# Recurrent branch of a hybrid layer: the chain's products on the full array instead of on half and quarter tiles

## The chip, the cores and the metric

One core of a Trainium2 chip. TensorE (PE) multiplies, VectorE (DVE), ScalarE (ACT) and GpSimd (POOL) work on what it leaves in PSUM, SyncE (SP) issues most transfers. The metric is the device time of one launch in microseconds; the time before is the median of three runs, 2056.92 us (2055.39 to 2056.93).

## The reference, cut to what matters

One layer of a decoder trunk of width 2048 over 288 tokens: 32 sample tokens (8 sequences of 4) and one prompt of 256. The norm of x goes through one input projection. Its columns feed two branches: RWKV-7 time mixing with 32 heads of 64 channels, and sliding-window attention. Gates merge the branches, and an output projection, a squared-ReLU MLP of width 8192 and a last norm follow. For each head the time mixing updates a 64 x 64 state S token by token:

```
sa  = S a_t                              (what is to be removed)
S   = S * w_t + v_t k_t^T + sa b_t^T     (decay, new value, removal)
y_t = S r_t
```

The outputs y are group-normalised per head, gain a bonus term and are gated. The states and the shifted columns of the last tokens are outputs as well. All inputs and outputs are float32.

## The kernel before

Channels lie on partitions, in 16 tiles of 128 (two heads each), and tokens along the free axis. `dense()` makes one output tile: a half tile of weights is loaded, split in two float32r parts by ScalarE (`whi`, L141) and VectorE (`wlo`, L142), and every contraction tile takes three products with 288 columns (L170 to L172). A half tile is thus 24 products. `whi` and `wlo` have two buffers each.

The recurrence goes in chunks of 64 prompt tokens, 4 of them, so that TensorE can do it. Two channel tiles are a group (GP = 2), and there are 8 groups. `pair()` prepares one channel tile: decayed and scaled copies of r, k, a and b (`T`, `bk`), coefficients within a chunk (L563), sample tokens (L579, L590). `chain()` works on a group: first VectorE inverts 32 x 32 triangular blocks by a recurrence on `A` and `utmp` (L625, L627), whose result goes out to DRAM and comes back (L641, `Y`, L659); small products on 32 x 32 tiles finish the inverse (`YT`, L664, L683); then the chunks follow one another:

- `za` (L721): states and values times the removal part of `T`, copied to `zs` by ScalarE (L723);
- `sa` (L732): the inverse times `zs`; VectorE scales it into `Z` (L735);
- `sn` (L739): the change of state; VectorE adds it to the state (L746) and decays it (L747), and ScalarE puts the result into the next chunk's `Z` (L751);
- the outputs gather in a PSUM bank `y` through L728 (old state) and L742 (within the chunk).

After four chunks the rows of y are centred (L702 to L705), squared, and scaled by GpSimd (L764), transposed back to channels (L771), and the sample states are updated (L787, L788). `finish()` adds bonus and gate (L809 to L814); its gate product (L184 to L186) uses the only bank of the small products (`ps_lo`).

The products of the chain take the two heads apart: 64 rows or 64 columns of the array for each head, as tiles of 128 x 64 and 64 x 64; L563 uses 64 x 128. Each of their instructions is two records in the trace, since the operands are float32.

The main loop (L327) issues `pair()` for one channel tile after another and after each of its steps three steps of side work (SIDE_STEPS), which is chain and finish of earlier groups; attention has its own pace. The order on every engine is then set once, when the program is built: a scheduler takes instructions of all these streams as their inputs and buffers come free. On the chip each engine's queue runs in that order.

Of the kernel before, what the change touches and what calls it, by code (L numbers as in the profile page):

```python
# [8 lines left out]
F32 = mybir.dt.float32  # L9
# [13 lines left out]
GP = 2  # L23
# [17 lines left out]
def _col_tiles():  # L41
    """Columns of w_in, tile by tile, and the index of each tile."""
# [30 lines left out]
def _consts():  # L73
# [5 lines left out]
    out["gmask"] = np.concatenate([s < t, s <= t], 1)  # L79
# [3 lines left out]
    out["smask"] = np.concatenate([same & (sp < tp), same & (sp <= tp)], 1)  # L83
    out["bmask"] = (sp // 4 == np.arange(8)[None, :])
# [40 lines left out]
class Builder:  # L125
# [21 lines left out]
    def weights(self, src):  # L147
        """One half tile [128, 1024] of weights, split in two float32r parts."""
# [29 lines left out]
    def lora(self, parts, out=None):  # L178
        """psum[128, NT] = sum of the parts (whi, wlo, xhi, xlo)."""
# [14 lines left out]
    def rstd(self, ps, out):  # L194
        """1 / sqrt(mean + eps) from the sums of squares in psum."""
# [6 lines left out]
    def build(self):  # L202
# [10 lines left out]
        self.ps_ch = self.pool("ps_ch", 2, PSUM)  # L213
        self.ps_y = self.pool("ps_y", 1, PSUM)
# [21 lines left out]
    def phase1(self, c1, ph):  # L236
# [9 lines left out]
        nc.gpsimd.dma_start(out=self.mu, in_=io["mu"])  # L246
        self.lhi = p1.tile([128, 4, NT], F32R, name="lhi")
        self.llo = p1.tile([128, 4, NT], F32R, name="llo")
        # the first tiles take x times the norm's weight, and the token's factor afterwards
        with ExitStack() as st:  # L250
# [9 lines left out]
            for q in range(8):  # L260
# [11 lines left out]
                # sums of squares: the first on the tensor engine, which waits for x anyhow  # L272
# [39 lines left out]
        nc.gpsimd.dma_start(out=self.sinks, in_=io["sinks"].partition_broadcast(128))  # L312
        self.srow = p1.tile([128, 4], F32, name="srow")
        nc.gpsimd.dma_start(out=self.srow, in_=io["srow"])
# [3 lines left out]
        self.GR = [p1.tile([128, 2, NCH, C], F32, name=f"GR{i}") for i in range(4)]  # L318
        for t in self.GR:
            nc.gpsimd.memset(t[64:128, 0], 0.0)  # L320
            nc.gpsimd.memset(t[0:64, 1], 0.0)
# [5 lines left out]
        for ct in range(KT):  # L327
# [9 lines left out]
            if 1 <= ct <= 4:  # L337
                # past rows of the sample V window
# [8 lines left out]
        # the rest of the gates, and the output projection over the first half of the channels  # L347
# [40 lines left out]
    def advance(self, side, n):  # L388
        """n steps of the side work; an item waits for the attention that it needs."""
# [8 lines left out]
    def shift(self, ps, name, tag, rstd=None):  # L398
        """Token shift of one tile of projected columns; also keeps the last tokens."""
# [35 lines left out]
    def group_begin(self, g):  # L435
# [5 lines left out]
        G.T, G.GB, G.GR, G.BKT, G.GS, G.Zs, G.bv, G.bkS = ([None] * GP for _ in range(8))  # L441
# [5 lines left out]
    def pair(self, G, p):  # L447
# [6 lines left out]
        # decay  # L454
# [22 lines left out]
        # a, k and the removal vectors  # L477
# [8 lines left out]
        # squared norms: by token for the chunks, along the columns for the sample tokens  # L486
# [23 lines left out]
        # scaled operands: rows of the second head hold k before b  # L510
        bk = ew.tile([128, NCH, 2, C], F32, name="bk")
        bks = ew.tile([128, 2, NS], F32, name="bks")
        T = G.T[p] = gp.tile([128, 2, NCH, 128], F32, name="T", bufs=4)
        ars = ew.tile([128, 2, NS], F32, name="ars", bufs=2)
        a8 = lambda i: ars[:, i, :].rearrange("p (b t) -> p b t", t=TS)
        hs = [slice(0, 64), slice(64, 128)]
        for h in range(2):
            r = hs[h]
# [605 lines left out]
```

## Time and profile before

| | |
|---|---|
| median of three runs | 2056.92 us |
| span of the profiled execution | 2052.3 us |
| TensorE busy | 1985.0 us (97%), 15732 records |
| VectorE busy | 1307.2 us (64%) |
| ScalarE busy | 948.5 us (46%) |
| GpSimd busy | 323.7 us (16%) |
| split of weights, L142, on VectorE | 621.3 us, 504 of 1234 ns |
| TensorE's waits for that split, 88 to 1140 us | 12.8 us, 19 of them, the longest 1.3 |

The recurrent branch and attention lie between some 88 and 1100 us, beside the dense products of the input projection; the output projection and the MLP follow. All times are of one profiled execution, whose span is 4.6 us under the median of the runs. The ends of products are modelled, so a price is read from start to start, over the dense products on both sides.

### The profile page before, as it was taken

Reading aid. Unit: us, or ns where it says so; the run is one execution under the profiler, and the core shown is the slowest. Engines: PE = TensorE matmul, PEld = TensorE weight load, DVE = VectorE, ACT = ScalarE, POOL = GpSimd, SP = SyncE. Lnnn points to the kernel's source line nnn. Section 1 sums busy time; section 2 is a strip of 40 time slices with the busy share of each in tenths; the row PEclk is TensorE's granted clock in tenths of the full one; section 3 lists DMA queues with packets and bytes.
Section 4 is the critical chain, followed back from the end, with each engine's and each line's share of the span. In section 5 each row is a group of like instructions: output and inputs, shape, how many; then the busy total and the mean of one; then the engine's idle time right before and its main releaser. Section 6 shows DMA issues by size and latency. Waiting matters only on the chain.

```text
span 2052.3 us, 39981 instructions
## 1 busy us (share of the span) xinstructions
PE 1985.0 (97%) x15732; PEld 1869.8 (91%) x15732; DVE 1307.2 (64%) x2594; ACT 948.5 (46%) x1801; POOL 323.7 (16%) x551
## 2 busy tenths in 40 slices
PE   6999999999999999899999999999999999999996
PEld 5998898988888888798888999999999999999996
DVE  8667768677686786977766684544554444444455
ACT  5545544545454454545444455433443344335442
POOL 6322213232141321414022000000000000000000
PEclk9999999999999999999999999999999999999998
DMA  5545455354553444445446655455545555555552
GB/s 195 162 145 166 124 157 162 115 167 130 151 167 111 143 148 147 135 141 161 127 137 197 192 163 166 159 173 166 165 158 172 164 165 162 167 165 165 165 166 96
DMA packets 156764, 319.21 MB, mean 156 GB/s; under 512 B 58208, under 2 KB 80768, under 8 KB 156512
## 3 DMA queue, kind: packets, MB, share of 16 engines
q1 hardware_dynamic: 156480, 316.61, 48.4%
q8 instruction: 124, 2.03, 0.4%
q14 instruction: 64, 0.52, 0.1%
q0 software_dynamic: 96, 0.05, 0.1%
HBM read 300.11 MB, written 18.52 MB: 155 GB/s over the span
## 4 chain that ended last, share of the span: by engine, by line
PE 72%; DVE 10%; DMA 3%; issue 2%; ACT 1%; POOL 1%; SPq 1%; DVEq 0%; ACTq 0%; POOLq 0%
PE mm L172 21%; PE mm L170 21%; PE mm L171 21%; DVE wlo L142 2%; DVE A L627 1%; DVE utmp L625 1%; PE gr L563 1%; PE y L742 1%; PE y L728 1%; DMA A<-scr 1%; PE gr L590 1%; PE ch L721 1%; PE ch L739 1%; PE ch L732 1%; PE lo L905 0%
## 5 line engine op out<-in xcount | busy, mean ns | idle before, releaser
L142 DVE TENSOR_TENSOR wlo<-raw,whi 128x1024 fp32r<-128x1024 f32 x504 | 621.3, 1234 | 461.0 <-ACT whi L141 455.9
L141 ACT CAST whi<-raw 128x1024 fp32r<-128x1024 f32 x504 | 528.2, 1050 | 728.8 <-PE mm L171 664.3
L172 PE MATMUL mm<-xhi,wlo 128*128 128x288 f32 x2304 | 694.6, 302 | 13.4 <-DVE wlo L142 13.3
L170 PE MATMUL mm<-xhi,whi 128*128 128x288 f32 x2304 | 690.8, 300 | 5.3 <-ACT bt L412 2.9
L171 PE MATMUL mm<-xlo,whi 128*128 128x288 f32 x2304 | 688.0, 299 | 0.0
L172 PEld LDWEIGHTS mm<-xhi,wlo 128*128 128x128 f32 x2304 | 435.2, 189 | 32.6 <-DVE wlo L142 18.2
L170 PEld LDWEIGHTS mm<-xhi,whi 128*128 128x128 f32 x2304 | 434.8, 189 | 17.0 <-issue 6.0
L171 PEld LDWEIGHTS mm<-xlo,whi 128*128 128x128 f32 x2304 | 434.7, 189 | 11.0 <-issue 8.7
L171 PE MATMUL mm<-ul,whi 128*128 128x288 f32 x1024 | 302.0, 295 | 0.0
L170 PE MATMUL mm<-uh,whi 128*128 128x288 f32 x1024 | 301.9, 295 | 0.0
L172 PE MATMUL mm<-uh,wlo 128*128 128x288 f32 x1024 | 301.5, 295 | 0.0
L172 PEld LDWEIGHTS mm<-uh,wlo 128*128 128x128 f32 x1024 | 192.7, 188 | 0.0
L170 PE MATMUL mm<-mhi,whi 128*128 128x288 f32 x640 | 189.6, 297 | 2.9 <-ACT mhi L144 1.8
L171 PEld LDWEIGHTS mm<-ul,whi 128*128 128x128 f32 x1024 | 192.2, 188 | 0.0
L170 PEld LDWEIGHTS mm<-uh,whi 128*128 128x128 f32 x1024 | 191.9, 187 | 0.0
L171 PE MATMUL mm<-mlo,whi 128*128 128x288 f32 x640 | 189.7, 296 | 0.2 <-DVE mlo L145 0.2
L172 PE MATMUL mm<-mhi,wlo 128*128 128x288 f32 x640 | 189.1, 296 | 0.7 <-DVE wlo L142 0.7
L1019 POOL TENSOR_TENSOR h<-h,rstd 128x288 f32<-128x288 f32 x5 | 4.9, 1013 | 910.7 <-DVE rstd L199 910.7
L170 PEld LDWEIGHTS mm<-mhi,whi 128*128 128x128 f32 x640 | 120.4, 188 | 4.2 <-ACT mhi L144 2.1
L172 PEld LDWEIGHTS mm<-mhi,wlo 128*128 128x128 f32 x640 | 121.0, 189 | 1.1 <-DVE wlo L142 1.0
L171 PEld LDWEIGHTS mm<-mlo,whi 128*128 128x128 f32 x640 | 120.7, 189 | 1.4 <-issue 0.8
L625 DVE TENSOR_TENSOR utmp<-A,U 108x84 f32<-108x84 f32 (+12 forms) x240 | 66.3, 276 | 18.7 <-DMA A<-scr 11.6
(303 smaller groups left out, 2344.1 us busy)
## 6 DMA issues: line engine op xcount, KB each, us to landing
raw<-win SPq DMA_DIRECT2D x216, 512.0 KB
raw<-wup SPq DMA_DIRECT2D x128, 512.0 KB
raw<-wdn SPq DMA_DIRECT2D x128, 512.0 KB
raw<-wout SPq DMA_DIRECT2D x32, 512.0 KB
S<-wkv SPq DMA_DIRECT2D x32, 256.0 KB
lraw<-lora SPq DMA_DIRECT2D x32, 128.0 KB
o_wkvs<-S SPq DMA_DIRECT2D x16, 256.0 KB
U<-scr SPq DMA_DIRECT2D x24, 144.0 KB
```

Source lines behind the costliest of these rows:

```text
L141: nc.scalar.copy(out=dst_hi, in_=src)
L142: nc.vector.tensor_tensor(out=dst_lo, in0=src, in1=dst_hi, op=ALU.subtract)
L170: nc.tensor.matmul(ps[:, :NT], lhsT=a, rhs=hi, start=(i == 0), stop=False)
L171: nc.tensor.matmul(ps[:, :NT], lhsT=a, rhs=lo, start=False, stop=False)
L172: nc.tensor.matmul(ps[:, :NT], lhsT=b, rhs=hi, start=False, stop=(i == len(kts) - 1))
L563: nc.tensor.matmul(grs[h][:, c, :], lhsT=bk[hs[h], c, :, :].rearrange("p a b -> p (a b)"), rhs=T[hs[h], h, c, :], start=True, stop=True)
L590: nc.tensor.matmul(rt[hs[h]], lhsT=ars[hs[h]].rearrange("p a b -> p (a b)"), rhs=S0[hs[h]], start=True, stop=True)
L625: nc.vector.tensor_tensor(out=tv, in0=A[:, 0:n, j:j + 1].broadcast_to([3 * NU, n, m]), in1=U[:, j:j + 1, j + 1:32].broadcast_to([3 * NU, n ...
L627: nc.vector.tensor_tensor(out=A[:, 0:n, j + 1:32], in0=A[:, 0:n, j + 1:32], in1=tv, op=ALU.add)
L721: nc.tensor.matmul(za[hs[h], p, :], lhsT=G.T[p][:, h, c, 0:64], rhs=Zc[:, h, p, :], start=True, stop=True)
L728: nc.tensor.matmul(y[half, cp, p, h, :], lhsT=G.T[p][:, h, c, 64:128], rhs=Zc[:, h, p, :], start=(cp == 0 and p == 0 and h == 0), stop=False)
L732: nc.tensor.matmul(sa[hs[h], p, :], lhsT=YT[hs[h], p, c, :], rhs=zs[hs[h], p, :], start=True, stop=True)
```

## The change

Every operand of the two heads becomes one block operand with zeros where the other head would be, and one product on the full array serves both. `T` holds removals and outputs of one chunk side by side, so that one product gives `za` and the old part of the outputs. `BG` holds the scaled b and k of a chunk beside the coefficients of the outputs, so that one product gives the change of state and the new part of the outputs. `YT`, `YS`, `abd`, `bbd` and `cbd` are block operands for the inverse, the sample tokens and the sample outputs. The outputs no longer gather in PSUM: `za` and `sn` each have a part of them, ScalarE copies one (`y1`, L760) and VectorE adds the other (`yt`, L761). The bank that was `y` becomes a third bank of the chain. GpSimd clears the new operands. Three small loads go from GpSimd's queue to SP's. The products L664 and L683 stay as they are. Lines from 576 on are 8 to 13 higher after the change. The core of the diff:

```diff
-        self.ps_ch = self.pool("ps_ch", 2, PSUM)
-        self.ps_y = self.pool("ps_y", 1, PSUM)
+        self.ps_ch = self.pool("ps_ch", 3, PSUM)
...
-        nc.gpsimd.dma_start(out=self.mu, in_=io["mu"])
+        nc.sync.dma_start(out=self.mu, in_=io["mu"])
...
+        self.BG = [p1.tile([128, NCH, 2, 2, C], F32, name=f"BG{i}") for i in range(4)]
...
+        for t in self.YT + self.YS + self.abd + self.bbd + [self.cbd]:
+            nc.gpsimd.memset(t, 0.0)
...
-        T = G.T[p] = gp.tile([128, 2, NCH, 128], F32, name="T", bufs=4)
+        T = G.T[p] = gp.tile([128, 2, NCH, 2, C], F32, name="T", bufs=4)
...
+            nc.gpsimd.memset(T[hs[1 - h], h], 0.0)
...
-        nc.scalar.copy(out=BKT, in_=tr)
+        for h in range(2):
+            nc.scalar.copy(out=BG[:, :, h, h, :], in_=tr[:, :, h, :])
...
-            za = bank64()
+            za = four(bank()[:, 0:GP * 128])
             for p in range(GP):
                 for h in range(2):
-                    nc.tensor.matmul(za[hs[h], p, :], lhsT=G.T[p][:, h, c, 0:64], rhs=Zc[:, h, p, :], start=True, stop=True)
+                    nc.tensor.matmul(za[:, p, h, :], lhsT=G.T[p][:, h, c].rearrange("q a b -> q (a b)"), rhs=Zc[:, h, p, :], start=True, stop=True)
             zs = gp.tile([128, GP, 64], F32, name="zs")
-            nc.scalar.copy(out=zs, in_=za)
+            for h in range(2):
+                nc.scalar.copy(out=zs[hs[h]], in_=za[hs[h], :, h, :])
             yield 0
             sa = bank64()
             for p in range(GP):
-                for h in range(2):
-                    nc.tensor.matmul(y[half, cp, p, h, :], lhsT=G.T[p][:, h, c, 64:128], rhs=Zc[:, h, p, :],
-                                     start=(cp == 0 and p == 0 and h == 0), stop=False)
...
-                    nc.tensor.matmul(sa[hs[h], p, :], lhsT=YT[hs[h], p, c, :], rhs=zs[hs[h], p, :], start=True, stop=True)
+                nc.tensor.matmul(sa[:, p, :], lhsT=YT[:, p, c].rearrange("q h t -> q (h t)"), rhs=zs[:, p, :], start=True, stop=True)
...
-                    nc.tensor.matmul(sn[hs[h], p, :], lhsT=G.BKT[p][:, c, hs[h]], rhs=Zc[:, h, p, :], start=True, stop=True)
-            for p in range(GP):
-                for h in range(2):
-                    nc.tensor.matmul(y[half, cp, p, h, :], lhsT=G.GR[p][:, h, c, :], rhs=Zc[:, h, p, :], start=False,
-                                     stop=(c >= 2 and p == GP - 1 and h == 1))
-            yield 0
+                    nc.tensor.matmul(sn[:, p, h, :], lhsT=G.BG[p][:, c, h].rearrange("q a b -> q (a b)"), rhs=Zc[:, h, p, :], start=True, stop=True)
             Sn = gp.tile([128, GP, 64], F32, name="Sm", bufs=2)
-            nc.vector.tensor_tensor(out=Sn, in0=sn, in1=Sm, op=ALU.add)
+            for h in range(2):
+                nc.vector.tensor_tensor(out=Sn[hs[h]], in0=sn[hs[h], :, h, :], in1=Sm[hs[h]], op=ALU.add)
...
+            y1 = gp.tile([128, GP, 64], F32, name="y1")
+            for h in range(2):
+                o = hs[1 - h]
+                nc.scalar.copy(out=y1[o], in_=za[o, :, h, :])
+                nc.vector.tensor_tensor(out=yt[half, cp, :, h, :], in0=sn[o, :, h, :], in1=y1[o], op=ALU.add)
             yield 0
...
-            for h in range(2):
-                nc.tensor.matmul(sn[hs[h]], lhsT=G.bkS[p][hs[h]], rhs=zm[hs[h]], start=True, stop=True)
+            nc.tensor.matmul(sn, lhsT=G.bkS[p], rhs=zm, start=True, stop=True)
```

The order of the queues changes with it. First place: TensorE's queue in the chain of the sixth group, before the change. `mm` is a dense product, `ch` and `y` are banks of the chain; a number belongs to one tile in memory.

```order
L170 MATMUL mm_11783<-xhi_93,whi_11786 128x288
L171 MATMUL mm_11783<-xlo_94,whi_11786 128x288
L739 MATMUL ch_11206<-Z_8434,BKT_8931 64x64 x2
L739 MATMUL ch_11206<-Z_8434,BKT_9798 64x64 x2
L742 MATMUL y_11043<-Z_8434,GR2_566 64x64 x2
L742 MATMUL y_11043<-Z_8434,GR3_567 64x64 x2
L172 MATMUL mm_11783<-xhi_93,wlo_11787 128x288
L170 MATMUL mm_11783<-xhi_93,whi_11786 128x288
```

After the change, the last two chunks of the same group, from the last dense product on:

```order
L173 MATMUL mm_12033<-xhi_90,wlo_12067 128x288
L731 MATMUL ch_10948<-Z_8566,T_8916 128x64 x2
L731 MATMUL ch_10948<-Z_8566,T_9784 128x64 x2
L738 MATMUL ch_10956<-zs_10953,YT1_574 128x64 x2
L746 MATMUL ch_11033<-Z_8566,BG2_563 128x64 x2
L746 MATMUL ch_11033<-Z_8566,BG3_564 128x64 x2
L731 MATMUL ch_11049<-Z_8567,T_8916 128x64 x2
L731 MATMUL ch_11049<-Z_8567,T_9784 128x64 x2
L738 MATMUL ch_11057<-zs_11054,YT1_574 128x64 x2
L746 MATMUL ch_11106<-Z_8567,BG2_563 128x64 x2
L746 MATMUL ch_11106<-Z_8567,BG3_564 128x64 x2
L782 MATMUL ch_11207<-cst_89,cen_10755 128x128 x2
```

Before, dense products stand on both sides of each step; after, two chunks and the transposes of the normalised rows stand behind one another, and the next dense product comes only behind L795, L783, L665, L675, L192 and a gate product.

Second place: VectorE's queue in the chain of the seventh group, before the change. `A` and `utmp` are the recurrence of the next group's inverse, `wlo` the split of a half tile of weights, `S` and `am` belong to attention.

```order
L142 TENSOR_TENSOR wlo_13297<-raw_13294,whi_13296 128x1024
L877 SCALAR_TENSOR_TENSOR S_13117<-cst_92,gr_13120 128x384
L627 TENSOR_TENSOR A_12935<-A_12935,utmp_13172 108x6x13
L735 TENSOR_TENSOR Z_10091<-ch_12614,RH_10093 64x128 x2
L878 TENSOR_REDUCE am_13118<-S_13117 128x2
L879 TENSOR_REDUCE am_13118<-S_13117 128x2
L625 TENSOR_TENSOR utmp_13175<-A_12935,U_12934 108x84
L882 TENSOR_SCALAR am_13118<-am_13118,sinks_558 128x2 x2
L627 TENSOR_TENSOR A_12935<-A_12935,utmp_13175 108x7x12
L883 TENSOR_SCALAR am_13118<-am_13118 128x4
L625 TENSOR_TENSOR utmp_13178<-A_12935,U_12934 108x77
L142 TENSOR_TENSOR wlo_13327<-raw_13324,whi_13326 128x1024
```

After the change, from the last split of weights ahead of the place at which that group's last chunk ends without dense products between its steps:

```order
L143 TENSOR_TENSOR wlo_13067<-raw_13064,whi_13066 128x1024
L642 TENSOR_TENSOR A_12571<-A_12571,utmp_12685 108x4x19
L740 TENSOR_TENSOR Z_10208<-ch_12282,RH_10210 64x128 x2
L640 TENSOR_TENSOR utmp_12688<-A_12571,U_12570 108x90
L642 TENSOR_TENSOR A_12571<-A_12571,utmp_12688 108x5x18
L640 TENSOR_TENSOR utmp_12691<-A_12571,U_12570 108x85
L642 TENSOR_TENSOR A_12571<-A_12571,utmp_12691 108x5x17
L640 TENSOR_TENSOR utmp_12694<-A_12571,U_12570 108x80
L749 TENSOR_TENSOR Sm_12292<-ch_12287,Sm_12191 64x128 x2
L761 TENSOR_TENSOR yt_11971<-ch_12287,y1_12297 64x2x64 x2
L642 TENSOR_TENSOR A_12571<-A_12571,utmp_12694 108x5x16
L750 TENSOR_TENSOR Sm_12292<-Sm_12292,DE_10209 128x128
```

Before, two splits stand 11 rows apart, with the recurrence, attention and the chain between them; after, the next split stands 69 rows behind the first row here, and in between are 37 instructions of the recurrence, the group's last chunk, its normalisation and the sample states. TensorE's queue there holds, between two dense products, L731, L738, L746, L782, L795, L783, L795, L665, L675, L605 and the first scores of attention (L845 to L881).

## Rows read from the trace of the kernel before

**Rows 1.** by stretch: length, then for each engine busy us and records; PEclk, DMA, GB/s

```profile
88.00:1140.00 1052.00, 1020.88 (x8567) 909.82 (x8567) 775.64 (x1909) 507.23 (x1163) 271.87 (x470) 0.99 0.48 148
...
1400.00:1600.00 200.00, 200.00 (x1505) 200.00 (x1504) 95.68 (x110) 83.27 (x111) 0.00 (x0) 1.00 0.51 166
```

**Rows 2.** timeline of TensorE, line 732: start, us, engine, line, out<-in, tile, sizes, records

```profile
1062.38 0.29 PE L171 MATMUL mm<-xlo,whi 128*128 128x288 f32 x1
1062.60 0.45 PE L732 MATMUL ch<-zs,YT 64*64 64x64 f32 x8
...
1063.22 0.29 PE L170 MATMUL mm<-xhi,whi 128*128 128x288 f32 x1
```

**Rows 3.** timeline of TensorE, lines 739 and 742

```profile
1080.37 0.29 PE L170 MATMUL mm<-xhi,whi 128*128 128x288 f32 x1
1080.59 0.45 PE L739 MATMUL ch<-Z,BKT 128*64 128x64 f32 x8
1080.88 0.63 PE L742 MATMUL y<-Z,GR 128*64 128x64 f32 x8
...
1081.68 0.29 PE L172 MATMUL mm<-xhi,wlo 128*128 128x288 f32 x1
```

**Rows 4.** timeline of TensorE, line 563

```profile
846.74 0.29 PE L172 MATMUL mm<-xhi,wlo 128*128 128x288 f32 x1
846.96 1.16 PE L563 MATMUL gr<-T,bk 64*128 64x128 f32 x8
...
848.28 0.29 PE L171 MATMUL mm<-xlo,whi 128*128 128x288 f32 x1
```

**Rows 5.** timeline of TensorE, line 787

```profile
309.15 0.29 PE L171 MATMUL mm<-xlo,whi 128*128 128x288 f32 x1
309.37 1.08 PE L787 MATMUL ch<-zm,bkS 64*64 64x512 f32 x4
...
310.61 0.29 PE L170 MATMUL mm<-xhi,whi 128*128 128x288 f32 x1
```

**Rows 6.** timeline of TensorE, line 902 on the full array

```profile
410.24 0.30 PE L171 MATMUL mm<-xlo,whi 128*128 128x288 f32 x1
410.38 0.71 PE L902 MATMUL gr<-cst,S 128*128 128x128 f32 x5
...
411.06 0.30 PE L170 MATMUL mm<-xhi,whi 128*128 128x288 f32 x1
```

**Rows 7.** costliest groups by line: busy us, mean ns of one, idle before

```profile
L142 DVE TENSOR_TENSOR wlo<-raw,whi 128x1024 fp32r<-128x1024 f32 x504 | 621.3, 1234 | 461.0 <-ACT whi L141 455.9
L627 DVE TENSOR_TENSOR A<-A,utmp 108x84 f32<-108x84 f32 (+12 forms) x240 | 68.0, 283 | 4.5
L625 DVE TENSOR_TENSOR utmp<-A,U 108x84 f32<-108x84 f32 (+12 forms) x240 | 66.3, 276 | 18.7 <-DMA A<-scr 11.6 <-issue 1.7 <-DMA U<-scr 0.9
L751 ACT COPY Z<-Sm 64x128 f32<-64x128 f32 x48 | 14.3, 298 | 21.7 <-DVE Sm L747 21.1
...
L746 DVE TENSOR_TENSOR Sm<-ch,Sm 128x128 f32<-128x128 f32 x32 | 9.2, 287 | 13.0 <-PE ch L739 12.7
```

**Rows 8.** chain that ended last, 600 to 640 us: start, us, what

```profile
599.43 1.78 SPq L641
...
604.01 0.43 DVE X L659
```

**Rows 9.** timeline of all engines in the tail

```profile
1096.54 1.08 PE L955 MATMUL lo<-pP,vp 128*128 128x32 f32 x8 [1.76 <-DMA vp<-cv]
...
1102.49 0.69 DVE L702 TENSOR_REDUCE gst<-y 128x8 f32<-128x512 f32 x1
...
1105.29 0.71 PE L170 MATMUL mm<-mhi,whi 128*128 128x288 f32 x2 [1.85 <-ACT mhi L144]
...
1110.61 1.26 POOL L764 TENSOR_TENSOR cen<-cen,gst 128x640 f32<-128x640 f32 x1 [1.70 <-DVE gst L763]
```

**Rows 10.** by stretch, in the tail; columns as in rows 1

```profile
1098.60:1102.00 3.40, 3.14 (x26) 2.70 (x27) 1.96 (x8) 0.41 (x1) 0.00 (x0) 0.51 0.44 125
```

More of the change, by code (lines that the diff above doesn't have):

```diff
@@ L78, in _consts @@
     s, t = (p % 64)[:, None], np.arange(64)[None, :]
-    out["gmask"] = np.concatenate([s < t, s <= t], 1)
+    out["gmask"] = np.concatenate([s < t, s <= t, s < t], 1)
     sp = (p % 32)[:, None]
@@ L83, in _consts @@
     out["smask"] = np.concatenate([same & (sp < tp), same & (sp <= tp)], 1)
+    out["sel"] = (p % 64)[:, None] == 32 + tp
     out["bmask"] = (sp // 4 == np.arange(8)[None, :])
@@ L440, in group_begin @@
         G.RH = gp.tile([128, GP, NCH], F32, name="RH", bufs=3)
-        G.T, G.GB, G.GR, G.BKT, G.GS, G.Zs, G.bv, G.bkS = ([None] * GP for _ in range(8))
+        G.T, G.GB, G.BG, G.GS, G.Zs, G.bv, G.bkS = ([None] * GP for _ in range(7))
         G.R = gp.tile([128, GP, 64], F32, name="R", bufs=3)
@@ L671, in chain @@
         for p in range(GP):
-            for h in range(2):
-                nc.tensor.matmul(sa[s32[h], p, :], lhsT=YS[s32[h], p, :], rhs=zs[s32[h], p, :], start=True, stop=True,
-                                 tile_position=(h * 64, h * 64))
+            nc.tensor.matmul(sa[:, p, :], lhsT=YS[:, p].rearrange("p h a -> p (h a)"), rhs=zs[:, p, :], start=True, stop=True)
         for p in range(GP):
@@ L682, in chain @@
                 for h in range(2):
-                    nc.tensor.matmul(qq[s32[h], p, c, :], lhsT=Pm[k32[h], p, c, :], rhs=YT[k32[h], p, c, 32:64], start=True, stop=True,
+                    nc.tensor.matmul(qq[s32[h], p, c, :], lhsT=Pm[k32[h], p, c, :], rhs=YT[k32[h], p, c, h, 32:64], start=True, stop=True,
                                      tile_position=(h * 64 + 32, h * 64))
         for h in range(2):
-            nc.scalar.copy(out=YT[s32[h], :, :, 32:64], in_=qq[s32[h]])
+            nc.scalar.copy(out=YT[s32[h], :, :, h, 32:64], in_=qq[s32[h]])
         yield 0
@@ L689, in chain @@
         for p in range(GP):
-            for h in range(2):
-                nc.tensor.matmul(yp[hs[h], p, :], lhsT=G.GS[p][hs[h]].rearrange("p a b -> p (a b)"), rhs=G.Zs[p][hs[h], :], start=True, stop=True)
+            nc.tensor.matmul(yp[:, p, :], lhsT=flat(G.GS[p]), rhs=G.Zs[p], start=True, stop=True)
         ys = gp.tile([128, GP, 64], F32, name="ys", tag="zs")
@@ L713, in chain @@
         nc.gpsimd.memset(Z[0][64:128, 1], 0.0)
-        y = self.ps_y.tile([128, NCH // 2, GP, 2, 64], F32, name="y")
+        yt = gp.tile([128, NCH // 2, GP, 2, 64], F32, name="yt")
+        four = lambda t: t.rearrange("q (p h i) -> q p h i", p=GP, h=2)
         for c in range(NCH):
@@ L763, in chain @@
         nc.vector.reciprocal(out=rs, in_=rs)
-        nc.gpsimd.tensor_tensor(out=cen, in0=cen, in1=rs.unsqueeze(2).broadcast_to([128, NR, 64]), op=ALU.mult)
+        n4 = 4 * GP
+        nc.gpsimd.tensor_tensor(out=cen[:, 0:n4], in0=cen[:, 0:n4], in1=rs[:, 0:n4].unsqueeze(2).broadcast_to([128, n4, 64]), op=ALU.mult)
+        for h in range(2):
+            nc.gpsimd.tensor_tensor(out=self.cbd[hs[h], :, h, :], in0=cen[hs[h], n4:NR], in1=rs[hs[h], n4:NR].unsqueeze(2).broadcast_to([64, GP, 64]), op=ALU.mult)
         yield 0
@@ L771, in chain @@
                 nc.tensor.transpose(tr[:, NS + cp * 128:NS + cp * 128 + 128], cen[:, o:o + 2, :].rearrange("q h i -> q (h i)"), ident)
-            for h in range(2):
-                nc.tensor.matmul(tr[hs[h], 0:NS], lhsT=cen[k32[h], 4 * GP + p, :], rhs=ident[k32[h], k32[h]], start=True, stop=True,
-                                 tile_position=(h * 64 + 32, h * 64))
+            nc.tensor.matmul(tr[:, 0:NS], lhsT=self.cbd[:, p].rearrange("q h i -> q (h i)"), rhs=self.c["sel"], start=True, stop=True)
             col = slice(g * GP + p, g * GP + p + 1)
```

109 lines of the change are left out of this document (55 added, 54 removed).

## Prediction

> **What bounds the kernel now.** I read the share of busy time by stretch first. In the recurrent stretch (88 to 1140 us) TensorE is busy 1020.9 of 1052 us and VectorE 775.6; in a stretch that holds dense products alone, 1505 of them fill 200 us without a gap, so one costs 133 ns from start to start [rows 1]. Nothing else is near its limit, so the change must be judged by what it takes out of or puts into TensorE's queue. That queue is in order and its order is fixed when the program is built: a product that waits holds up everything behind it, dense products included. I therefore read, second, the timeline of TensorE around single steps of the chain, to get the price of one step with all that it does to its neighbours; third, the rows of the engines between the steps; and fourth, the one place of before where chain steps stand with hardly any dense product between them (1094 to 1106 us), as a sample of what such a place costs.
>
> **What TensorE's own work becomes.** In each group of rows the first row is the last dense product before a step, and the last row is the second dense product behind it; between them lies one dense product that the dots leave out. Of the time from the first start to the last, two dense products are 0.27 us, and the rest is the price of the step.
> - Removal product on 64 x 64 tiles, 8 records: 1063.22 - 1062.38 = 0.84, price 0.57 us [rows 2].
> - State change with outputs, 16 records: 1081.68 - 1080.37 = 1.31, price 1.04 us [rows 3]. The removals with the old part of the outputs have the same tiles and 16 records too, and I give them the same 1.04.
> - Coefficients, 8 records of 64 x 128: 848.28 - 846.74 = 1.54, price 1.27 us [rows 4].
> - Sample state change, 4 records with 512 columns: 310.61 - 309.15 = 1.46, price 1.19 us [rows 5]. The sample products of line 590 have the same form.
> - Five records on the full array: 411.06 - 410.24 = 0.82, price 0.55 us, which is 0.11 us for one, and nothing is lost on entering or leaving [rows 6].
>
> One chunk before: 1.04 + 0.57 + 1.04 = 2.65 us. After: 4 + 2 + 4 products, 20 records of 0.11 = 2.2 us. No row has full-array records with 64 columns; the bounds are the same 0.11 (if the weights set the pace) and half of it (if the columns did, against the 128 of the row). I take 0.11, the row's, and -0.45 x 32 chunks = -14.4 us. Coefficients: 8 x 0.11 = 0.88 for 1.27, 32 times, -12.5 us. The sample products of lines 590 and 787: two full-array records with 512 columns. No row shows one. From below it costs 0.27 us, a fourth of the 1.08 that the four records of the row take; from above 4 x 0.11 = 0.44, four times the 128 columns of rows 6. I take the upper: 0.88 for 1.19, 16 + 16 times, -9.9 us. The small sample steps (lines 579, 652, 673, 691, 773) fall from about 0.57 to 0.44 for a step, about 32 steps, -4. Together -41. Where steps stood side by side in before, they shared the entry and the exit, which takes a little back: I take **-39 us**, with -30 to -50 as its ends.
>
> The rule that speaks against this part: rows 2 hold 8 tile records at 0.57 us, where 8 full-array records are 0.88, so a single product does become dearer, and it is cheaper only because one now does the work of two (1.04). The Trainium skill, "TensorEngine Tiling (Array Packing)", section "Theoretical Speedup", says that tiles give up to twice the speed where a dimension is at most 64. By it alone, full products would double the 2.65 us of a chunk and add 85 us; the row bears out a factor of 1.5 for one product, not for the pair.
>
> **Two places where the order exposes the chain.** The changed order has two runs of chain steps with no dense product between them. At both the next half tile of weights but one is not split yet, and its split, which stands ahead in VectorE's queue, waits for TensorE to leave the buffer, that is for the dense product at which the run begins. So VectorE cannot have run ahead: its work starts when TensorE's dense work stops.
> - Second place (one chunk, normalisation, sample state, then the inverse's first use of the next group). VectorE's queue from the split on: the split, 1.23 us; 37 instructions of the recurrence on A at 0.28 = 10.4; seven operations of the chain at 0.29 = 2.0; four passes over wider tiles at 0.69 = 2.8; small ones 1.1; together 17.5 us [rows 7, 9]. Then A goes out and comes back: 604.01 - 599.43 = 4.6 us, and two transposes of 0.43 [rows 8]. That makes 23 us with no wait. The waits for the copies, the normalisation on GpSimd and the state product add about 2, and the products that then stand before the next dense one about 3: 28 us, in which TensorE works 8. Idle **20 us** (15 to 24).
> - First place (two chunks, normalisation, sample state, gate product). A chunk by hand-overs: products 0.88 + 0.44 + 0.88, four copies of 0.30, seven VectorE operations of 0.29, together 5.4 us. Two of them 10.8; the split ahead 1.2; pieces of the recurrence that stand in VectorE's queue on the way, 3; the normalisation 7 (in the tail it took 9.4 us from 1102.49 to 1111.87 with other work in the queues [rows 9]); then transposes, the channel scaling, the gate's addition, which must free the only bank of the small products, the bonus sum and six gate products, 4. That is 26 us, TensorE busy 10. Idle **16 us** (10 to 20).
> - Behind each place the next split is late once: 2 us together (0 to 6).
> - The clock: in the stretch from 1098.6 us, right after 1.8 us of waiting at line 955, the granted clock was 0.51 for 3.4 us, which is the 1.2 GHz level, and again from 1105.5 [rows 9, 10]. Two long idle places should bring several such stretches, on the chain's products and on the first dense ones: **+5 us** (2 to 10).
>
> **The rest.** VectorE gets 64 additions of outputs and 32 more for the state, 96 x 0.29 = 28 us, and some 5 us of small ones [rows 7]; this is 775.6 to 809 us in a stretch of about the same length. Most of it runs beside dense products; the part at which splits become late I put at **+5 us** (0 to 15). ScalarE and GpSimd get some 30 and 37 us of copies and clearing, and have the room for it. The tail of before lost 1.8 us at line 955 and 1.9 at line 170 [rows 9]; after, 14, 24 and 47 dense products stand between those steps: **-4 us** (-6 to 0). Of the three loads moved to SP's queue one now stands ahead of x; the issues of line 641 take 1.78 us together [rows 8], so it costs less than that, and I take nothing, since TensorE at the start waits for the first weights as well.
>
> **Sum.** 2052.3 - 39 + 16 + 20 + 2 + 5 + 5 - 4 = 2057.3 us for the profiled execution. The median of the runs is 4.6 us above the span of before's profile, so **2062 us**, 0.25% slower.
>
> **Rivals.**
> - The runs are filled (faster). If VectorE reached them with the recurrence mostly done, only the hand-overs would be left, about half the idle time, and the clock would stay up: -18 - 4, so 2040 us. It decides at the split that waits: if its buffer is free 10 us earlier, VectorE is that far ahead. For it: VectorE is idle a quarter of the stretch [rows 1]. Against: two buffers and the order. Chance 0.23.
> - The two sides cancel (no change): idle time as forecast, but without late splits and with half the clock's loss: 2062 - 7 = 2055 us. Chance 0.25.
> - VectorE becomes the bound (slower still): the 33 us added come in the middle of the groups, where it is busy more than its mean of 74%; if 20 of them show: 2062 + 15 = 2077 us. For it: every half tile needs 1.23 of its 3.2 us for the split [rows 7]. Against: what stands between two splits hardly changes outside the two places. Chance 0.15.
> - Full-array products are dearer than 0.11 us with 64 columns or with zeros in them: 0.15 each would add 0.8 us to a chunk and 0.3 to the coefficients, 35 us in all: 2097 us. Against: rows 6, where 128 columns cost 0.11. Chance 0.02. The rule of the Trainium skill on tiles, above, leans this way.
> - The change does not do what it says: the inverse's products on 32 x 32 tiles and attention's tiles stay, and so do the changes of tile there. That is counted.
>
> **How the numbers follow.** Forecast 2062 with 0.35. About 0.2%, or 4 us, can be told from no change, and 2061 is where slower begins. Slower: most of the forecast's chance (0.33), the third rival and the fourth: 0.50. Same: the forecast's lower edge (0.02) and the second rival but for 0.01: 0.26. Faster: the first rival and that 0.01: 0.24. The forecast's own range is 2054 to 2072. The range to hold 8 times in 10 takes in most of the first and the third rival: 2043 to 2082.
>
> **What would show it.** Right: TensorE's busy time falls by about 35 us or more, with dense starts 133 ns apart on both sides of a chunk's products and 0.88 us for the new removal product; and two idle stretches of 15 us or more in TensorE's rows, in the sixth and seventh of the eight groups, ended by the chain, with a granted clock of 0.5 inside. Wrong: removal products of 1.2 us or more; no idle place over 5 us between 850 and 1040 us; or waits for the split of weights that grow from group to group. A time under 2050 us would say that the idle places were filled; over 2075, that VectorE ran out of room.

## The result, and the profile after

The changed kernel takes 2117.91 us (2117.34 to 2118.15), 1.03 times the kernel before (95% interval 1.0285 to 1.0314). The forecast was 2062 us, between 2043 and 2082: the sign was right, the size was not: 3% slower for the 0.25% forecast.

The page of the changed kernel: TensorE works 6 us less, in a span that is 63.8 us longer.

```profile
span 2116.1 us, 38576 instructions
...
PE 1978.7 (94%) x14868; PEld 1904.2 (90%) x14868; DVE 1347.8 (64%) x2714; ACT 967.5 (46%) x1899; POOL 338.4 (16%) x653
```

The prices of the new products that can be read are those of the prediction. TensorE's timeline, changed kernel, the removal product with the old outputs alone between dense products: 668.72 - 667.56, less 0.27 for two dense products, is 0.89 us for 8 records. That is 0.11 us for one, as for the records of [rows 6].

```profile
667.56 0.29 PE L172 MATMUL mm<-xlo,whi 128*128 128x288 f32 x1
667.69 1.00 PE L731 MATMUL ch<-Z,T 128*128 128x64 f32 x8
...
668.72 0.29 PE L171 MATMUL mm<-xhi,whi 128*128 128x288 f32 x1
```

And the coefficients, 389.61 - 388.44 less 0.27, which is 0.90 us for the 1.27 of [rows 4]:

```profile
388.44 0.30 PE L172 MATMUL mm<-xlo,whi 128*128 128x288 f32 x1
388.58 1.05 PE L576 MATMUL gr<-T,bk 128*128 128x128 f32 x8
...
389.61 0.29 PE L171 MATMUL mm<-xhi,whi 128*128 128x288 f32 x1
```

Two records with 512 columns take 0.86 us from start to start, 0.43 each, near the upper bound of 0.44:

```profile
964.01 1.02 PE L605 MATMUL gr<-S,abd 128*128 128x512 f32 x2
964.87 0.38 PE L543 MATMUL gr<-cst,vx 128*128 128x128 f32 x2
```

To see where the time went I count half tiles by their splits on VectorE (L143, before L142), which are the same 504 in both programs. Split 180 starts at 906.2 us after and 906.1 before: up to there nothing is won or lost. Split 200 starts at 1075.5 and 1004.0: here 71 us are lost. After that nearly 8 us come back. The two stretches between splits 20, 180 and 200 (columns as in [rows 1]), changed kernel first, then before:

```profile
97.30:906.20 808.90, 764.07 (x5879) 714.06 (x5878) 616.60 (x1541) 400.64 (x967) 219.55 (x449) 0.99 0.46 143
906.20:1075.50 169.30, 125.14 (x878) 113.15 (x878) 117.21 (x324) 63.39 (x157) 40.51 (x74) 0.81 0.35 103
```

```profile
96.60:906.10 809.50, 785.09 (x6521) 701.40 (x6519) 605.57 (x1504) 395.01 (x919) 217.82 (x398) 0.99 0.47 145
906.10:1004.00 97.90, 97.54 (x878) 86.68 (x877) 75.59 (x186) 48.10 (x108) 25.10 (x40) 1.00 0.49 150
```

Two things are to be read. In the long first stretch TensorE works 764.1 instead of 785.1 us, and stands idle for 44.8 instead of 24.4: the products are 21 us shorter and the waits 20 us longer. In the short one it is idle for 44.2 instead of 0.4 us, and the granted clock falls from 1.00 to 0.81. In the trace, 64.9 us of that stretch were at the 1.2 GHz level, and TensorE worked for 33.4 us of them. At 2.4 GHz that work would have taken about half as long (an estimate: dense products start 0.24 us apart at the low level, below, for 0.133), so the low clock cost some 17 us there.

The waits of TensorE between 88 and 1200 us, changed kernel (total us, times, longest): the split is waited for twice as long as before (12.8), and the three other waits shown lie in the two places, all of the first and the third and 8.6 us of the second.

```profile
PE mm L173 <- DVE wlo L143: 25.9, 24, 2.9
PE ch L782 <- POOL cen L773: 16.0, 2, 8.3
PE ch L675 <- DVE X L670: 9.6, 4, 7.5
...
PE gr L605 <- DMA S<-wkv: 3.9, 1, 3.9
```

The first place, TensorE (columns as in [rows 2]; the idle time before a row and what ended it in brackets):

```profile
925.20 1.00 PE L731 MATMUL ch<-Z,T 128*128 128x64 f32 x8
...
945.69 1.12 PE L782 MATMUL ch<-cst,cen 128*128 128x128 f32 x4 [7.69 <-POOL cen L773]
...
958.33 0.61 PE L171 MATMUL mm<-xhi,whi 128*128 128x288 f32 x1
```

From the chain's first product to the next dense one it takes 33.1 us for the 26 predicted. The waits between its rows add up to 14.9 us, for 16; TensorE is busy for 18 us and not 10.

The second place, all engines:

```profile
1031.36 1.00 PE L731 MATMUL ch<-Z,T 128*128 128x64 f32 x8
...
1032.55 1.23 DVE L143 TENSOR_TENSOR wlo<-raw,whi 128x1024 fp32r<-128x1024 f32 x1 [0.29 <-ACT whi L142]
...
1040.76 0.23 DVE L640 TENSOR_TENSOR utmp<-A,U 108x84 f32<-108x84 f32 x1
...
1040.93 1.05 POOL L792 TENSOR_TENSOR zm<-Zs,cst 128x512 f32<-128x512 f32 x1 [4.13 <-DVE gst L768]
1041.03 1.05 DVE L642 TENSOR_TENSOR A<-A,utmp 108x84 f32<-108x84 f32 x1
...
1043.66 1.12 PE L782 MATMUL ch<-cst,cen 128*128 128x128 f32 x4 [8.27 <-POOL cen L773]
...
1044.57 1.92 PE L795 MATMUL ch<-zm,bkS 128*128 128x512 f32 x2
...
1049.71 0.34 SPq L798 DMA_DIRECT2D o_wkvs<-S  x1
...
1052.22 1.31 SPq L648 DMA_DIRECT2D scr<-A  x3
1053.64 0.36 SPq L790 DMA_DIRECT2D S<-wkv  x1
...
1056.48 0.69 DVE L796 TENSOR_TENSOR S<-ch,S 128x512 f32<-128x512 f32 x1 [4.29 <-DMA S<-wkv]
...
1057.66 0.28 PE L675 MATMUL ch<-X,GB 32*32 32x32 f32 x2 [7.46 <-DVE X L670]
...
1058.32 0.36 SPq L798 DMA_DIRECT2D o_wkvs<-S  x1
1058.61 0.43 DVE L670 STREAM_TRANSPOSE X<-Y 32x256 f32<-32x256 f32 x1 [1.10 <-DMA Y<-scr]
...
1061.45 0.35 SPq L603 DMA_DIRECT2D S<-wkv  x1
...
1064.10 2.07 PE L605 MATMUL gr<-S,abd 128*128 128x512 f32 x2 [3.93 <-DMA S<-wkv]
...
1069.31 0.61 PE L171 MATMUL mm<-xhi,whi 128*128 128x288 f32 x1
```

The dense products stop at 1031.4 and go on at 1069.3 us, 38 us for the 28 predicted; the waits add up to 24.4 us, for 20. VectorE's split starts at 1032.55, when ScalarE has filled the buffer that TensorE has just left, as predicted. From there to the end of the inverse at 1052.2 VectorE needs 19.7 us for the 17.5 of the sum. Part of this is that single instructions of the recurrence take about 1 us and not 0.25 while an operation of GpSimd runs (1041.03 beside 1040.93). In this trace 37 of the recurrence's 480 instructions take over 0.6 us, and each of them overlaps with one of GpSimd.

Behind the inverse stand two things that the sum did not have. First, `S0`, the sample state of one channel tile, has one buffer. The first tile of the group is stored at 1049.71; the load of the second goes out at 1053.64, behind the inverse's transfer in SP's queue (L648), and VectorE waits 4.29 us for it at L796. TensorE loses little by that wait alone, since the second transpose of `X`, which stands behind it, waits for its own load until 1058.61. But the tile must then be stored as well (1058.32) before the next load into the buffer (1061.45), and that load holds up L605 for 3.9 us. Second, the products run at the low clock: the two records of L795 at 1044.57 take 1.70 us to the next product at 1046.27, for the 0.86 of L605 above. In the first place the low clock lasts for 30.7 us without a break, and the dense products at its end start 0.24 us apart:

```profile
931.20:961.90 30.70, 18.95 (x91) 14.90 (x92) 15.03 (x45) 8.20 (x18) 12.87 (x25) 0.50 0.23 62
```

```profile
959.69 0.44 PE L173 MATMUL mm<-xhi,wlo 128*128 128x288 f32 x1
959.93 0.44 PE L171 MATMUL mm<-xhi,whi 128*128 128x288 f32 x1
```

### The profile page after: what moved, and what is told of

The parts are those of the page before. It is cut to its first block, busy times and chain, and to the rows that moved or that the text cites. A ratio compares the mean times of both kernels' runs of the same rounds, so it can differ in the third digit from the quotient of the medians.

```text
span 2116.1 us, 38576 instructions
## 1 busy us (share of the span) xinstructions
PE 1978.7 (94%) x14868; PEld 1904.2 (90%) x14868; DVE 1347.8 (64%) x2714; ACT 967.5 (46%) x1899; POOL 338.4 (16%) x653
## 4 chain that ended last, share of the span: by engine, by line
PE 67%; DVE 14%; DMA 5%; issue 2%; ACT 2%; SPq 1%; POOL 0%; DVEq 0%; POOLq 0%; ACTq 0%
PE mm L171 19%; PE mm L173 19%; PE mm L172 19%; DVE wlo L143 3%; DVE utmp L640 1%; DVE A L642 1%; PE gr L576 1%; PE ch L731 1%; DMA A<-scr 1%; PE ch L746 1%; DMA S<-wkv 1%; DMA o_wkvs<-S 1%; DMA scr<-GS 1%; DVE T L531 1%; ACT whi L142 0%
## 5 line engine op out<-in xcount | busy, mean ns | idle before, releaser
L143 DVE TENSOR_TENSOR wlo<-raw,whi 128x1024 fp32r<-128x1024 f32 x504 | 619.3, 1230 | 435.9 <-ACT whi L142 430.0
L142 ACT CAST whi<-raw 128x1024 fp32r<-128x1024 f32 x504 | 527.4, 1047 | 699.5 <-PE mm L172 617.4
L640 DVE TENSOR_TENSOR utmp<-A,U 108x84 f32<-108x84 f32 (+12 forms) x240 | 64.9, 270 | 28.8 <-DMA A<-scr 23.3
```

Of the source, the lines that this page charges most:

```text
L142: nc.scalar.copy(out=dst_hi, in_=src)
L143: nc.vector.tensor_tensor(out=dst_lo, in0=src, in1=dst_hi, op=ALU.subtract)
L640: nc.vector.tensor_tensor(out=tv, in0=A[:, 0:n, j:j + 1].broadcast_to([3 * NU, n, m]), in1=U[:, j:j + 1, j + 1:32].broadcast_to([3 * NU, n ...
```

## The experiments

Times are medians; ratios are to the kernel before, with 95% intervals. "Stretch" is splits 20 to 200: 907.4 us before, with 24.8 idle.

**The order or the products.** In the tile kernel a chunk of the chain has four steps of side work, in the changed one three, since two kinds of products became one. A group offers 42 side steps (14 yields of three). Chain and gates have 38 + 4 yields before and 34 + 4 after, and the call that finds a generator at its end uses a step too, so they ask for 44 steps before and for 40 after. The yield by itself, both ways round:

```diff
(full array)
+            yield 0
             Sn = gp.tile([128, GP, 64], F32, name="Sm", bufs=2)
...
(tiles)
-            yield 0
             Sn = gp.tile([128, GP, 64], F32, name="Sm", bufs=2)
```

> The changed kernel with one more yield in each chunk (between the state-change product and the addition to the state), so that a chunk takes four steps of side work as before the change. Same products and operands, other order. Theory A (the loss is the order: a chunk of three steps lets the chain run into two places without dense products): no idle place of 20 us or more near 925 and 1030 us, a short one at half tile 198, time 2045 to 2068 us. Theory B (the loss is the form of the products: longer latencies, more copies and additions between them): 2100 us or more.

> The kernel before the change with one yield fewer in each chunk (the one behind the state-change and output products), so that its tile products get the pace of the changed kernel. Theory A: the same two places behind half tiles 184 and 198, each some 30 us idle with the first dense product after them, time 2110 to 2135 us. Theory B: within 10 us of 2056.

| | four steps | three steps |
|---|---|---|
| tiles | 2056.2 us | 2109.9 us, 1.0256 (1.0233 to 1.0279) |
| full array | 2058.1 us, 1.0016 (1.0002 to 1.003) | 2117.9 us, 1.03 |

The full-array kernel with four steps, by splits 20, 180, 200:

```profile
97.20:902.00 804.80, 767.54 (x5933) 716.87 (x5932) 633.84 (x1584) 405.00 (x983) 227.30 (x463) 0.99 0.47 146
902.00:1006.00 104.00, 98.26 (x766) 93.31 (x766) 79.32 (x207) 52.23 (x127) 26.77 (x50) 0.97 0.47 141
```

The tile kernel with three:

```profile
97.60:903.10 805.50, 779.04 (x6491) 696.70 (x6489) 592.74 (x1461) 390.69 (x907) 209.66 (x388) 0.99 0.47 145
903.10:1061.30 158.20, 126.35 (x1052) 103.24 (x1051) 109.93 (x296) 58.57 (x133) 34.03 (x58) 0.83 0.36 107
```

The yield decides, in either kernel: 54 us with tiles (the time is just under the 2110 us expected), 60 with full-array products. The second rows, compared with the second of before: 5.7 us idle with four steps against 31.8 with three, clock 0.97 against 0.83. Theory A, the order, holds; the new form of the products, with the copies and additions that come with it, is worth about nothing, a little less than nothing by the interval.

**The one buffer of S0.** In the three-step kernel, then with four steps, at both places where `S0` is made:

```diff
-        S0 = gp.tile([128, NB, 64], F32, name="S0", bufs=1)
+        S0 = gp.tile([128, NB, 64], F32, name="S0", bufs=2)
...
-            S0 = gp.tile([128, NB, 64], F32, name="S0", bufs=1)
+            S0 = gp.tile([128, NB, 64], F32, name="S0", bufs=2)
```

> The changed kernel with two buffers for the sample state S0 instead of one; three steps in a chunk as changed, both places still in the order. If the store, load, store, load of the one buffer lies on the path in the second place (4.3 us in which VectorE waited for the load, 3.9 us in which TensorE did): 2105 to 2112 us. If other waits end there anyway: 2116 to 2120 us. Theory A keeps two long idle places in both cases.

> Both edits: four steps in a chunk and two buffers for S0. Theory A: as the kernel with four steps alone, less 0 to 5 us: 2040 to 2066 us. Theory B: 2095 us or more.

Measured 2099.9 us (1.0206, 1.0179 to 1.0233) and 2049.7 (0.9965, 0.9952 to 0.9979). So the second buffer was worth 18 us with the idle places, twice what I expected, and 8 without, where I expected 5 at most. Most of the 18 do not come from the two places: between the two profiles, 8.3 us lie between splits 20 and 180 and 3.9 between 180 and 200, where the idle time falls from 44.2 to 38.9 us. The long place stays (splits 180 to 200, two buffers, three steps), and in it TensorE still waits for a load of the sample state, which goes out only among the inverse's transfers (L648, at 1046.2 us):

```profile
897.40:1062.90 165.50, 126.54 (x863) 114.48 (x863) 116.79 (x326) 61.80 (x154) 40.13 (x72) 0.79 0.34 100
```

```profile
1049.61 2.07 PE L605 MATMUL gr<-S,abd 128*128 128x512 f32 x2 [4.74 <-DMA S<-wkv]
```

No run has two buffers of `S0` in the tile kernel, so what they are worth there is not known.

**VectorE's load.** The same base, four steps and two buffers, once without the additions of the outputs and once with each done twice:

```diff
-            y1 = gp.tile([128, GP, 64], F32, name="y1")
...
-                nc.scalar.copy(out=y1[o], in_=za[o, :, h, :])
-                nc.vector.tensor_tensor(out=yt[half, cp, :, h, :], in0=sn[o, :, h, :], in1=y1[o], op=ALU.add)
+                nc.scalar.copy(out=yt[half, cp, :, h, :], in_=za[o, :, h, :])
```

> The kernel with four steps in a chunk and two S0 buffers (2049.7 us, 0.9965 of before), with VectorE's 64 additions of the outputs left out: ScalarE's copies of the old part go straight into yt, so the new part of the outputs is missing from the prompt's rows. Theory C (the product time saved is eaten because VectorE, with 33 us more, splits the weights late): VectorE 19 us lighter, TensorE's waits for the split fall from 24 towards 12 us, and half tiles 20 to 200 take 8 to 15 us less (889 to 896 for 904). Theory D (VectorE's load does not matter there; the saved time goes to hand-overs and other waits): 900 us or more, split waits stay near 24. The tail differs in order (the last group's transposes come right behind its last chunk), so the stretch counts, not the end.

> The same base with each of the 64 additions of the outputs done twice (19 us more on VectorE, same result). Theory C: 8 to 15 us more in half tiles 20 to 200 (912 to 919 us for 904), split waits up by a similar size. Theory D: within 4 us of 904.

The stretch in the base, without the additions, and with two of each:

```profile
98.40:1002.30 903.90, 861.13 (x6690) 806.42 (x6688) 715.24 (x1787) 456.54 (x1109) 251.76 (x513) 0.99 0.47 145
```

```profile
98.50:1002.60 904.10, 861.61 (x6685) 804.25 (x6684) 701.08 (x1751) 458.12 (x1110) 257.21 (x513) 0.99 0.46 145
```

```profile
97.00:1009.30 912.30, 867.98 (x6694) 813.45 (x6693) 729.46 (x1841) 455.98 (x1102) 253.69 (x513) 0.98 0.46 144
```

VectorE falls by 14 us or rises by 14, and TensorE's idle time stays at 42.8, 42.5 and 44.3. Without the additions nothing is gained in the stretch, and TensorE's waits for splits between 88 and 1140 us go from 24.7 to 20.8 us and not towards 12 (whole kernel 2044.8 us, 0.9945, where the tail's order differs too). With two of each, 8 us are lost in the stretch, as theory C expected, but not for its reason: the waits for splits are 14.0 us, less than in the base, while 34.1 us of the stretch are at the low clock for 13.7 in the base. The whole kernel loses 15 us (2064.6, 1.0038, 1.0023 to 1.0053): in the profiles another 13 are lost between splits 200 and 240. So theory C, that VectorE's added load eats the saved time, falls by the run without the additions. Still more load does cost time, mostly in the tail, and no run here shows how.

**The coefficients alone.** Line 576 back on half-array tiles:

```diff
-                nc.tensor.matmul(grs[h][:, c, :], lhsT=bk[:, c].rearrange("p a b -> p (a b)"),
-                                 rhs=T[:, h, c].rearrange("p a b -> p (a b)"), start=True, stop=True)
+                nc.tensor.matmul(grs[h][:, c, :], lhsT=bk[hs[h], c].rearrange("p a b -> p (a b)"),
+                                 rhs=T[hs[h], h, c].rearrange("p a b -> p (a b)"), start=True, stop=True)
```

> The same base with the 256 products of the coefficients (line 576) back on 64 x 128 tiles, as before the change; operands otherwise unchanged. By the prediction's term (1.27 for 0.88 us, 32 times): TensorE busy and the time up by 12 us, to 2062. If steps that stand side by side share the entry and exit, and waits take up the rest: busy up by 3 to 8 us, time 2049 to 2056 us.

2058.0 us (1.0008, 0.999 to 1.0026), 8 us more, and TensorE's busy time is up by 16. But the profiled execution had 37.5 us of the stretch at the low clock, the base 13.7. With the work in those counted at half, an estimate, splits 20 to 240 take 6 us more work: half of the predicted 12.5.

**The buffers of the split.** In the base TensorE waits 24.7 us for splits, and in all of these waits but the one at 90.7 us ScalarE's part was ready and VectorE busy with something else. One of them:

```profile
831.89 1.03 ACT L142 CAST whi<-raw 128x1024 fp32r<-128x1024 f32 x1
...
835.83 1.27 DVE L537 SCALAR_TENSOR_TENSOR abd<-kx,E 64x32 f32<-64x32 f32 x2
...
838.25 1.16 DVE L143 TENSOR_TENSOR wlo<-raw,whi 128x1024 fp32r<-128x1024 f32 x1
...
839.46 0.40 PE L173 MATMUL mm<-xhi,wlo 128*128 128x288 f32 x1 [3.35 <-DVE wlo L143]
```

ScalarE's cast for this half tile is done at 832.92. VectorE has work of `pair()` and more in its queue ahead of the split, which starts 5.3 us later, at 838.25; TensorE waited 3.35 us. The edits were of this kind, with one load buffer given up for each buffer added (here a third one for the high part; the tail's lists of buffers change with them):

```diff
-        self.wraw = [self.pool("wraw", 4)]
-        self.whi = [self.pool("whi", 2)]
-        self.wlo = [self.pool("wlo", 2)]
+        self.wraw = [self.pool("wraw", 3)]
+        self.whi = [self.pool("whi", 3)]
+        self.wlo = [self.pool("wlo", 2)]
```

> The kernel with four steps in a chunk and two S0 buffers (0.9965 of before), with three buffers for the low part of the weights instead of two, and three for the raw weights instead of four. Theory E (bursts of VectorE's other work stand ahead of single splits; the total is no limit): a split can run a half tile further ahead, TensorE's waits for splits between half tiles 20 and 200 fall from 24 to under 12 us, the stretch from 904 to 888 to 897, the time to 2030 to 2043 us. Rival F (ScalarE's part, whose buffers stay at two, or other hand-overs end the same waits): 900 us or more, time within 5 us of 2049.

> The kernel before with the same buffers (three for the low part, three raw), as the control. It waits 11.7 us for splits between half tiles 20 and 240. Theory E: 2 to 8 us faster, less than the full-array kernel gains from it. Rival F: within 3 us of 2056.

> The same base (four steps in a chunk, two S0 buffers; 0.9965 of before) with three buffers each for the high and the low part of the weights, and two for the raw ones. In every wait for a split so far ScalarE's part was done and VectorE was busy with other work. Theory G (a split has only the 3.2 us of one half tile in which it can be done, since ScalarE's part has two buffers, and bursts of other work fall into it): with both parts a half tile further ahead, waits for splits fall from 24 to under 12 us, half tiles 20 to 200 from 904 to 886 to 897 us, time 2030 to 2043 us. Rival H (the order of VectorE's queue is planned so tightly that more room changes nothing, or two raw buffers make the loads late): 900 us or more, with waits for raw weights if it is the loads.

> The same base with three buffers for the high part, two for the low part, three raw. Theory G: half of the gain, since the low part still waits for TensorE to leave its buffer but no longer for ScalarE: waits for splits 12 to 20 us, half tiles 20 to 200 in 893 to 902 us. Rival H: 902 us or more, waits 22 us or more.

> The kernel before with three buffers for the high part of the weights, two for the low part, three raw: the control for the same edit on the full-array kernel (0.9901 with two S0 buffers). It waits 12 us for splits. Theory G: at most those 12 us come off, 2045 to 2054 us, so that the full-array products are worth some 10 us once the splits are out of the way. Rival: the buffers alone give the whole gain, 2036 to 2042 us, and the full-array products nothing.

| buffers raw, high, low | full array, four steps, two S0 | tiles |
|---|---|---|
| 4, 2, 2 | 0.9965 | 1 |
| 3, 2, 3 | 0.995 (0.9935 to 0.9964) | 0.9997 (0.9987 to 1.0007) |
| 2, 3, 3 | 0.9907 (0.989 to 0.9925) | not run |
| 3, 3, 2 | 0.9901 (0.9885 to 0.9918) | 0.989 (0.9874 to 0.9907) |

A third low part changes nothing (theory E, the low part's buffer, falls). A third high part takes 12 us off the full-array kernel, and TensorE's waits for splits go from 24.7 us to 7.6 (theory G, the high part's buffer). With three low parts beside they go to none, but the time does not follow (0.9907 for 0.9901). And the control gained more than either theory expected: tiles with three high parts need 2032.9 us, 22 less than the kernel before and the best of all, where the waits for splits fell only from 12.8 to 7.1 us. In its stretch the idle time is 8.7 us less than before and TensorE's busy time 6.6 us less, and split 20 comes 3.8 us earlier. So theory G is not the whole of it. The stretch of that kernel, and of the full-array one with the same buffers and two of `S0`:

```profile
92.80:985.00 892.20, 876.07 (x7383) 785.08 (x7382) 684.48 (x1679) 440.34 (x1019) 234.64 (x438) 0.99 0.48 147
```

```profile
95.80:994.80 899.00, 858.69 (x6666) 807.64 (x6665) 713.22 (x1774) 457.44 (x1109) 249.30 (x513) 0.98 0.47 146
```

The full-array kernel works 17 us less and is idle for 24 us more.

**Product time alone.** Is it the added copies, additions and clearing that bring the waits, or does any product time saved turn into waits? The tile kernel without the output products within the chunks, with old and with new buffers:

```diff
-            for p in range(GP):
-                for h in range(2):
-                    nc.tensor.matmul(y[half, cp, p, h, :], lhsT=G.GR[p][:, h, c, :], rhs=Zc[:, h, p, :], start=False,
-                                     stop=(c >= 2 and p == GP - 1 and h == 1))
...
```

> The kernel before with the 128 output products within the chunks (line 742) left out, so the prompt's rows lack that part: about 15 us less for TensorE (0.47 of 1.04 us, 32 times), and no work added anywhere. Theory I (the idle time of the full-array kernel comes with the copies, additions and clearing that it adds on other engines): the time falls by 10 to 15 us, to 2041 to 2046, idle between half tiles 20 and 200 stays within 5 us of 24.8. Theory J (the other engines' hand-overs set the pace beside the dense products, and a shorter product only makes TensorE wait): 0 to 6 us, idle up by 10 or more.

> The same products left out of the tile kernel with three buffers for the high part of the weights (2032.9 us, 0.989). Theory I: 10 to 15 us less, 2018 to 2023 us, idle near 16. Theory J: 0 to 6 us less, 2027 to 2033 us, idle up by 10 or more.

2055.8 us (1.0, 0.9986 to 1.0013) and 2035.8 (0.9899, 0.9878 to 0.992): nothing, and nothing. The first one's stretch:

```profile
97.20:999.10 901.90, 869.18 (x7190) 772.91 (x7188) 677.85 (x1677) 439.26 (x1020) 240.30 (x438) 1.00 0.48 146
```

TensorE works 13 us less there and is idle for 8 us more (32.7); of the 5.5 us left, 3.8 are given back by split 240. With the new buffers TensorE works 6.3 us less in the stretch and is idle for 3.4 more; by split 240 nothing of the gain is left. The times fit theory J, by which product time taken away turns into waits, the idle time only in part. What sets the pace beside the dense products in the end, and so which waits take the place of each other, stays open: no run here shows it.

## Why the prediction was wrong

- **The step that failed most: the prices of the two places, 16 + 20 us idle, 2 for late splits and 5 us of clock.** The places were the right ones, and so was the reason that VectorE cannot run ahead (the split at 1032.55). Between splits 180 and 200 they cost 71 us: 44 more of idle time, some 17 of work at the low clock (half of 33.4), and 11 of other work, which had moved there: between splits 200 and 220 TensorE works 11 us less than before (102.1 for 113.1). The idle time was short by 6 us. The first place has 14.9 us of it for 16, the second 24.4 for 20, and there 3.9 us are the wait of L605 behind the one buffer of `S0`: its store and load I had not put into the walk, though lines 586 and 780 give it `bufs=1`. With two buffers the stretch has 38.9 us idle. The clock was short by a factor of three, because I took the length of a single stretch of [rows 10] and counted a few. In the first place the low level began 6 us after the dense products stopped and lasted for 30.7 us, with 19 us of work in it.
- **The product term, -39 us.** The prices that the changed profile shows were right, and the sum was not. That 0.11 us holds for products was luck in part: [rows 6] are transposes (L902), whose price I took over. With the work at the low clock counted at half, work between splits 20 and 240 fell by 25 us. For the coefficients, undone alone, it was 6 and not 12.5. The prices come from steps that stand alone between dense products. I think that in the order before many stand beside other tile work and share the entry and exit. I had taken 2 us off for it and should have counted; I have not counted since, so this reason is not shown.
- **The rest, +5 us.** Outside the two places the time saved in products was lost again to waits: 20 us up to split 180, 11 of them for splits (22.7 us for 11.7). I had put it down to VectorE's load, from its 33 us more. The run with 14 us less shows that this load is not the cause, and the runs with output products left out show that product time taken away can disappear without any load added. The cause itself stays open. The Trainium skill, "Perfetto Trace Analysis", section "Optimization Strategy", says that a gap which repeats on the engine that should be saturated can mean too few buffers. This case agrees: with a third buffer for the high part, the waits for splits fell from 24.7 to 7.6 us; a third for the low part left them at 24.2.
- **The tail, -4 us.** It did not shrink: the two waits of [rows 9], for the load of `vp` and for `mhi`, 1.8 us each, are now 2.8 and 3.6, and between splits 200 and 220 TensorE is idle for 9.9 us, 4.1 before. Waits of TensorE behind split 200, changed kernel (us in total, times, longest):

```profile
PE mm L171 <- ACT mhi L145: 3.6, 1, 3.6
PE lo L963 <- DMA vp<-cv: 2.8, 1, 2.8
```

- **The rivals and the signs.** Nothing like the "filled" runs came. The third, VectorE as the bound, had the right sign for the wrong cause, and so the sign set for a time over 2075 us, that VectorE ran out of room, pointed the wrong way. Dear full-array records were refuted: 0.89 us. Of the signs of being right, the idle places came with their clock and the 0.89, but TensorE's busy time fell by 6 us and not by 35, since the low clock took back most of it.
- **What I left out altogether** was why the order changed. I read the two places as given with the change. They come from one yield fewer in a chunk, which can be read in the code: 42 side steps offered, 44 asked for before, 40 after.

## What to carry to other kernels

Where a scheduler fixes the order, an edit that merges two steps also changes the pace at which side work is handed out; keep the number of yields, or test the yield by itself, before judging the new form of the products. Price an idle place with everything that its engines still have to fetch and store through single buffers, and with the low clock for most of its length, as in the first place here. And shorten the engine that is 97% busy only with a look at what it will wait for next: 25 us of product time were worth nothing here, while a third buffer for the high part of the weights, at the cost of one load buffer, was worth 22 in the tile kernel.

## What the runs showed of the hardware

The granted clock stayed at its lower level for as long as 30.7 us in one piece in the changed kernel (931.2 to 961.9 us), while TensorE was busy for 19 us of it, first with chain products that wait for one another and at the end with dense products that start 0.24 us apart. In the tile kernel with three steps the longest piece was 34.1 us (1022.3 to 1056.4); in the recurrent stretch of before none was longer than 3.4 us. A record on the full array costs 0.11 us with 64 columns as with the 128 of [rows 6], and 0.43 with 512 (L605). An instruction of the recurrence on VectorE takes at most 0.26 us where no operation of GpSimd overlaps with it, and up to 1.1 us where one does (changed kernel, 480 instructions).
